# One encoder layer on one core: matmul operands moved to multiples of 256 bytes, sums of weights and ready blocks issued at other places

## The chip, the cores and the metric

One Trainium2 chip, of which the kernel uses one core. The metric is the device time of one execution in microseconds (us). TensorE (PE), VectorE (DVE), ScalarE (ACT), GpSimd (POOL) and SyncE (SP, here a DMA queue) run their own instruction streams.

## The reference

One layer of an encoder with 512 tokens of 2048 channels, in fp32:

```python
h = rms_norm(x, pre_mix)
z = h @ w_in                              # q | k | v | u, 1024 columns each
a = chunked_attention(q, k, v, rel_bias)  # 8 heads of 128, chunks of 64, own chunk and 8 before
p = pooled(u) - u, a linear map per group, a scale per channel   # trailing means over 2, 4, 8, 16
x = x + rms_norm(concat(a, p) @ w_o, post_mix)
h = rms_norm(x, pre_ffn)
up = dwconv3(h @ w_up)                    # 2 x 5632 columns
x = x + rms_norm((gelu(up[:, :5632]) * up[:, 5632:]) @ w_down, post_ffn)
```

## The kernel before

Every fp32 matrix product is made of matmuls in a reduced fp32 format: `split` (L138) writes an operand as a rounded part (ACT, L140, names ending in h) and a rest (DVE, L141, names ending in l). `mm3` (L161) multiplies rounded by rounded, rounded by rest and rest by rounded; `mm2` (L167) does the same with one 512-wide matmul (L170) and one 256-wide matmul (L176) for two halves packed in one operand, all eight wide ones of a product and then all eight narrow ones, or in the other order for products that are "turned".

Large products go by a scheme with seven products of sums of blocks in place of eight. It needs sums of weight blocks and sums of activations. The stages, in time: q and k of the first head, to 31 us; half of v; q and k of heads 1 to 7 by seven products each (class Pairs, L432), to about 205 us, whose activation sums s5, s3, s6 lie in pool `ph`; then attention head by head between the second half of v, u and the pooling, to about 400 us; w_o by seven products (`wo_product`, L848, order 1, 7, 2, 5, 6, 3, 4, each twice for `cc` 0 and 1, in four quarters `q`); three blocks of w_up in the plain way; from about 632 to 1438 us the other 41 blocks of w_up by seven products (class Factors, L1320), whose activation sums h5, h3, h6 (`h` in the profile) lie in a pool named `ps` and whose plain factors `gT` lie in `big`; from 1438 us w_down by seven products in chunks (`multiply`, L1147), whose right factors `bh`, `bl` lie partly in pool `p4`, partly in pool `pr`; and a last block `yl`, from 1827 us.

Pools are laid out by a stack from the left and one from the right of the 128 partitions' memory. `place` (L100) allocates a tile that nothing reads, to shift all that comes behind it in its stack. Where matmul operands lie in the built program, as byte address in the partition modulo 256: `big` (the weights' parts `w4`, the plain factors, the factors of w_o), `p4`, `acc` and `p1`'s attention tiles at 128; `ps`, `pr` and `p1`'s `dh` at 0; `ph` at 224. Of 9564 matmuls, 6158 have both operands at 128, 3070 have the moving one at 0 and the stationary one at 128, 336 have the moving one at 224 and the stationary one at 128. The factors in `ps`, `pr` and `ph` are moving operands.

The order on PE is that of the code. The other engines are ordered by a scheduler, in which program order, buffers and `issue_after` count. `weights` (class Weights, L55) loads blocks through SP (L152) and splits them a few blocks ahead of their use.

The sums of weights for w_o and for the first chunk of w_down are made in DRAM by DMA alone, in `sums_in_dram` (L290): 48 steps, each a copy (L301 on POOL, L304 on SP) or an adding transfer (L308 on POOL) of 1 MB; steps 1 to 32 are for w_o, 33 to 48 for w_down. `more_sums(n)` takes the next n steps where the code calls it. While `more_sums.paced` is set, the copies too go through POOL's queue, and each step is held back by a memset on DVE (L295) and one on POOL (L296), so that it starts at that place in time. Step 6 is taken in the first half of v, 26 by the end of q and k, 28, 30 and 32 by the ends of heads 0, 1 and 2, 43 by the end of u, 46 in w_o and 48 in w_up.

Six blocks of w_down's first chunk are split ahead of time, in w_o (`ready_block`, L837): load a block `rw` through SP (L840), split it (`rwh`, L843) and store both parts in DRAM (L846). Each of the products 5, 6 and 3 of w_o starts one at its first quarter, both for `cc` 0 and 1, loads it behind quarter 0, splits it behind quarter 2 and stores it behind quarter 3.

Of the kernel before, what the change touches and what calls it, by code (L numbers as in the profile page):

```python
# [9 lines left out]
F32 = mybir.dt.float32  # L10
F32R = mybir.dt.float32r
# [4 lines left out]
P = 128  # L16
# [18 lines left out]
PAD = 16  # L35
# [10 lines left out]
def f32(ap):  # L46
    return ap.bitcast(F32)
# [34 lines left out]
def encoder_layer(ctx: ExitStack, tc: tile.TileContext, x, xT, vecs, rel, post_mix, post_ffn,  # L82
# [7 lines left out]
    nc = tc.nc  # L90
    ctx.enter_context(tc.manual_schedule(engines={mybir.EngineType.PE}))

    const = ctx.enter_context(tc.tile_pool(name="const", bufs=1))
# [6 lines left out]
    def place(pool, n):  # L100

        pool.tile([P, n // 4], F32, tag="place", bufs=1, name="place")

    place(const, 224)

    def bank(name):
        return psum.tile([P, 512], F32, tag="ps", name=name)
# [30 lines left out]
    def split(hi, lo, src, scale=None):  # L138
        if scale is None:
            rounded = nc.scalar.activation(hi, src, AF.Copy)  # L140
            rest = nc.vector.tensor_sub(lo, src, f32(hi))  # L141
        else:
            rounded = nc.scalar.activation(hi, src, AF.Copy, scale=scale)
            rest = nc.vector.scalar_tensor_tensor(lo, src, scale, f32(hi), op0=ALU.mult, op1=ALU.subtract)
        split.last, split.rest = rounded.ins, rest.ins
        return rounded.ins
# [109 lines left out]
    def first_block(cc, j, l):  # L256
        cs = slice(l * D // 2 + cc * S, l * D // 2 + (cc + 1) * S)
        return w_down[:2 * P * CU, cs].rearrange("(u j p) n -> p u j n", j=2, p=P)[:, :, j, :]

    READY = (0, 1), (1, 1), (0, 2)  # L260
    ready_w = {at: [dram.tile([P, CU, S], F32, name=f"rw{at[0]}{at[1]}{p}") for p in "hl"] for at in READY}

    ready_parts = [(at, j) for at in READY for j in range(2)]
# [65 lines left out]
    def more_sums(n):  # L329
        for _ in range(n):  # L330
            next(sums_step, None)
# [6 lines left out]
    rt = const.tile([P, NT], F32, name="rt")  # L338
    T = S // 2
    hsum, early_x, mixing_w = (ctx.enter_context(ExitStack()) for _ in range(3))  # L340
    ph = hsum.enter_context(tc.tile_pool(name="ph", bufs=1, side="right", reuse_waits="tile"))
    px = early_x.enter_context(tc.tile_pool(name="px", bufs=1, reuse_waits="tile"))
    ms = {i: ph.tile([P, 8, 2, T], F32R, tag=f"s{i}", name=f"s{i}") for i in (5, 3, 6)}
# [7 lines left out]
    for kb in range(KD):  # L351
        i, o = divmod(kb, 8)
        nc.sync.dma_start(xt[kb // 4][:, kb % 4, :], xT[kb * P:(kb + 1) * P, :])
        for n, what in enumerate("qk"):
            if kb in chunks:
                raw, hi, lo = first[f"{what}0_{i}"]
# [5 lines left out]
        for what in "qk":  # L362
            _, hi, lo = first[f"{what}0_{i}"]
# [132 lines left out]
    pairs = Pairs()  # L496
    psv = [bank(f"v0_{t}") for t in range(NT)]
    sums_of_x = x_sums()
    for n, _ in enumerate(v_steps(0, psv)):
        if n in (3, 5, 7, 9, 11, 13):  # L500
            more_sums(1)
        for _ in range(2):
            next(sums_of_x, None)
        if n == 9:
            for i, v in enumerate(differences):
                split(*(hT[i][:, :, at, :] for at in AT[1]), v)
            early_x.close()
            p0 = mixing_w.enter_context(tc.tile_pool(name="p0", bufs=1, reuse_waits="tile"))
# [75 lines left out]
    for k, i in [at for at in pairs.order if at[0] is not None]:  # L584
        if k == pairs.n - 1 and i in (7, 4):
            if not steps:
                psv = [bank(f"v1_{t}") for t in range(NT)]
                steps = v_steps(1, psv)
            next(steps)
        qk_product(k, i)  # L590
        qk_keep(k, i)
        if (k, i) == pairs.order[2]:
            spread1()
        if (k, i) == (pairs.n - 1, 7):
            restore()
            state["z", 0] = raw4("zq0").rearrange("p (a b) -> p a b", a=2)
            nc.sync.dma_start(state["z", 0], zqk[0])
            state["bias", 0] = raw4("bias0")[:, :S]
            restore.last = nc.sync.dma_start(state["bias", 0], rel[0]).ins
        if i in ((3, 7, 4) if k < pairs.n - 1 else (7, 4)):  # L600
            more_sums(1)

    hsum.close()
# [8 lines left out]
    with tc.tile_pool(name="p1", bufs=2, reuse_waits="tile") as p1:  # L612
# [110 lines left out]
        def pool_keep(g, j, ps):  # L723
            w = WINDOWS[g]
            u = p1.tile([P, WIDE], F32, tag="u", bufs=1, name="u")[:, :PAD + S]
            nc.vector.memset(u[:, :PAD], 0.0)
            nc.vector.tensor_mul(u[:, PAD:], ps, R)
            cur, step = u, 1
            while step < w:
                nxt = p1.tile([P, WIDE], F32, tag="us", bufs=2, name="us")[:, :PAD + S]  # L730
                nc.vector.tensor_add(nxt[:, step:], cur[:, step:], cur[:, :PAD + S - step])
                if 2 * step < w:
                    nc.vector.memset(nxt[:, :step], 0.0)
                cur, step = nxt, 2 * step
            edge = p1.tile([P, PAD], F32, tag="uf", bufs=2, name="uf")
            nc.vector.tensor_mul(edge, cur[:, PAD:2 * PAD], recip[:, g, :])
            d = t512("tmp", bufs=1)
            nc.vector.tensor_sub(d[:, :PAD], edge, u[:, PAD:2 * PAD])
            nc.vector.scalar_tensor_tensor(d[:, PAD:], cur[:, 2 * PAD:], 1.0 / w, u[:, 2 * PAD:],
                                           op0=ALU.mult, op1=ALU.subtract)  # L740
            hi, lo = t512(f"dh{j}", F32R, 1), t512(f"dl{j}", F32R, 1)
            split(hi, lo, d)
            state["pool", g, j] = hi, lo
# [25 lines left out]
        for h in range(3):  # L769
            if not h:  # L770
                run(2)
                ready_head(0)
            run(1)
            scores(h)
            more_sums(1)
            run(1)
            if h:
                values(h - 1)
            more_sums(1)
            run(1)  # L780
            ready_head(h + 1)
            run(1)
            turn(h)
            if not h:
                v_ready()
# [3 lines left out]
        def mid(h):  # L789
            def step():  # L790
                values(h)
                more_sums(1)
                if h == 2:
                    scores(3)
                elif h + 2 < HEADS:
                    ready_head(h + 2)
                if h == 3:
                    v_load(1)
            return step

        for j in range(8):
            ps = project(f"u{j}", mid(2 if j == 0 else j + 1) if j not in (1, 7) else None)
            if j == 0:
                ready_head(4)
            if j == 2:
                v_ready()
            if 1 <= j <= 5:
                turn(j + 2)
                if j < 5:
                    scores(j + 3)  # L810
            if j in (2, 4, 6):
                pool_mix(j // 2 - 1, spill_mix)
            if j < 7:
                pool_keep(j // 2, j % 2, ps)
                more_sums(1 if j in (0, 1, 3, 5, 6) else 0)
        u7 = ps
        more_sums.paced = False
        weights.ahead = 4
# [15 lines left out]
                split(*(w[:, 4 * i:4 * i + 4, :] for w in parts), v)  # L834
            return parts

        def ready_block(at, j):  # L837
            v, hi = (p2.tile([P, 1024], dt, tag=tag, name=tag) for tag, dt in (("rw", F32), ("rwh", F32R)))
            lo = v.bitcast(F32R)
            nc.sync.dma_start(v.rearrange("p (a b) -> p a b", a=2), first_block(at[0], at[1] - 1, 0)[:, 2 * j:2 * j + 2, :])  # L840
            yield
            yield
            split(hi, lo, v)  # L843
            yield
            for dest, part_ in zip(ready_w[at], (hi, lo)):
                nc.sync.dma_start(dest[:, 2 * j:2 * j + 2, :], f32(part_).rearrange("p (a b) -> p a b", a=2))  # L846

        def wo_product(i, cc, left, between=None):  # L848
            ps = [bank(f"m{i}{cc}{t}") for t in range(2)]
            if cc and i in (1, 5, 6):  # L850
                more_sums(1)
            ready = ready_block(*ready_parts.pop(0)) if i in (5, 6, 3) else iter(())
            for q in range(4):
                w = weights.get(f"wo{i}_{cc}_{q}")
                for j in range(2):
                    kb = 2 * q + j
                    for t in range(2):
                        mm3(ps[t], tuple(v[:, kb, t * P:(t + 1) * P] for v in left), part(w, j), kb == 0, kb == 7)
                next(ready, None)
                if between:  # L860
                    between(q)
            return ps
# [12 lines left out]
    with tc.tile_pool(name="p2", bufs=1, reuse_waits="tile") as p2:  # L875
# [164 lines left out]
                gate_part(q - 1, 2)  # L1040
                weights.prefetch(q)
        keep_x(2, turn_back.last)
        more_sums.paced = True
        for q in range(4):
            w = weights.get(f"w10_{q}")
            if q in (0, 2):
                more_sums(1)
            for kb in range(4 * q, 4 * q + 4):
                for j in range(2):
                    mm3(ups[1][j], part(w, j, slice(kb % 4 * P, (kb % 4 + 1) * P)), g_both(hT, kb),  # L1050
                        kb == 0, kb == KD - 1)
# [443 lines left out]
    with tc.tile_pool(name="p4", bufs=2, reuse_waits="tile") as p4:  # L1495
# [68 lines left out]
        ready = []  # L1564
# [111 lines left out]
        for n in ("11", "12", "21", "22"):  # L1676
            for t in range(2):
                at = y[t + 2 * int(n[0]) - 2]
# [64 lines left out]
```

## Time and profile before

| | us |
|---|---|
| median of 3 runs | 1878.97 |
| lowest and highest | 1877.44, 1880.14 |
| the profiled execution | 1881.62 |
| its span, first to last instruction | 1879.9 |

The mean granted clock of TensorE is 0.998 of full. In the timeline, a row has the start, the duration, the engine, the line, the operation, out<-in, sizes and count; in brackets the engine's idle time ahead and what ended it. The start-to-start distance of two PE rows, divided by the matmuls between them, is the rate of PE; the duration of one is longer than that, since matmuls overlap. A row of the chain has a start, a duration and the work. Groups of a tile have the lowest, median and highest duration in ns, and the first and last start.

### The profile page before, as it was taken

The numbers are of one execution on the slowest core, as the hardware profiler recorded it, in microseconds if no ns is written. First come the engines' busy times: TensorE is split into PE (matmuls) and PEld (weight loads), VectorE is DVE, ScalarE is ACT, GpSimd is POOL, SyncE is SP. The second block draws the span as 40 slices with busy tenths as digits, with TensorE's granted clock in tenths as the row PEclk, the third lists the DMA queues.
The fourth block names the chain that finished last, engine by engine and source line by source line (L and its number), as shares of the span: only waits on it lengthen the run. The fifth ranks groups of instructions, "written<-read, shape, count | busy, mean of one in ns | idle before, by whom it ended". The sixth has DMA issues, their size and how long they took to land.

```text
span 1879.9 us, 25452 instructions
## 1 busy us (share of the span) xinstructions
PE 1860.0 (99%) x9598; PEld 1584.6 (84%) x9598; DVE 1539.7 (82%) x1805; ACT 1082.1 (58%) x1376; POOL 303.3 (16%) x403
## 2 busy tenths in 40 slices
PE   9999999999999999999999999999999999999998
PEld 7888878887888888888888888888888888888886
DVE  6987767887698988888888888888888899898876
ACT  8655454556565656666566665656655655555453
POOL 3311110000000121212212122121121011111101
PEclk9999999999999999999999999999999999999999
DMA  7699997798985888888888988898888967777785
GB/s 284 193 319 305 311 267 213 225 251 300 347 297 183 213 197 199 206 207 200 196 197 206 208 196 197 202 207 207 195 177 297 360 215 160 192 212 170 171 238 143
DMA packets 139338, 426.01 MB, mean 227 GB/s; under 512 B 11920, under 2 KB 15376, under 8 KB 133520
## 3 DMA queue, kind: packets, MB, share of 16 engines
q0 software_dynamic: 54864, 173.56, 46.1%
q1 hardware_dynamic: 84352, 250.84, 38.1%
q8 instruction: 75, 1.23, 0.3%
q14 instruction: 47, 0.39, 0.1%
HBM read 370.35 MB, written 104.33 MB: 253 GB/s over the span
## 4 chain that ended last, share of the span: by engine, by line
PE 88%; DMA 4%; DVE 4%; ACT 2%; issue 1%; SPq 0%; POOL 0%; DVEq 0%; POOLq 0%; ACTq 0%
PE qa L170 18%; PE qa L176 9%; PE qg L170 9%; PE qg L176 5%; PE qd L170 4%; PE pa L162 4%; PE pa L164 4%; PE pa L165 4%; PE qd L176 2%; PE pg L162 2%; PE pg L164 2%; PE pg L165 2%; PE m L164 2%; PE m L165 2%; PE m L162 2%; PE u L162 1%
## 5 line engine op out<-in xcount | busy, mean ns | idle before, releaser
L140 ACT ACTIVATE wfh<-wx 128x1024 fp32r<-128x1024 f32 x192 | 203.6, 1060 | 151.7 <-PE qg L170 57.6
L170 PE MATMUL qa<-gT,wfh 128*128 128x512 f32 x1152 | 289.1, 393 | 0.0
L141 DVE TENSOR_TENSOR wfl<-wx,wfh 128x1024 fp32r<-128x1024 f32 x192 | 234.7, 1223 | 64.0 <-ACT wfh L140 46.7
L170 PEld LDWEIGHTS qa<-gT,wfh 128*128 128x128 f32 x1152 | 207.0, 188 | 37.5
L1360 POOL DMA_DIRECT2D wx<-in_w_up x122 | 104.6, 857 | 498.6 <-DVE wfl L141 468.3
L140 ACT ACTIVATE wfh<-wy 128x1024 fp32r<-128x1024 f32 x96 | 101.9, 1061 | 120.1 <-PE qg L170 62.4
L170 PE MATMUL qg<-h,wfh 128*128 128x512 f32 x656 | 165.7, 394 | 0.0
L176 PE MATMUL qa<-gT,wfl 128*128 128x256 f32 x1152 | 160.8, 282 | 1.7 <-ACT zm L1420 1.7
L176 PEld LDWEIGHTS qa<-gT,wfl 128*128 128x128 f32 x1152 | 151.0, 190 | 6.5 <-ACT zm L1420 2.1
L170 PEld LDWEIGHTS qg<-h,wfh 128*128 128x128 f32 x656 | 122.9, 188 | 28.0
L141 DVE TENSOR_TENSOR bl<-b,bh 128x2048 fp32r<-128x2048 f32 x56 | 127.3, 2287 | 22.5 <-ACT bh L140 11.7
L140 ACT ACTIVATE bh<-b 128x2048 fp32r<-128x2048 f32 x56 | 105.8, 1912 | 49.2 <-DVE b L1118 20.5
L141 DVE TENSOR_TENSOR wfl<-wy,wfh 128x1024 fp32r<-128x1024 f32 x96 | 117.2, 1221 | 13.3 <-ACT wfh L140 6.5
L162 PE MATMUL pa<-bh,ah 128*128 128x512 f32 x320 | 126.1, 394 | 0.0
L164 PE MATMUL pa<-bl,ah 128*128 128x512 f32 x320 | 125.8, 393 | 0.0
L165 PE MATMUL pa<-bh,al 128*128 128x512 f32 x320 | 125.5, 392 | 0.0
L141 DVE TENSOR_TENSOR wfl<-wz,wfh 128x1024 fp32r<-128x1024 f32 x48 | 58.7, 1224 | 53.7 <-PE qa L170 52.5
L176 PEld LDWEIGHTS qg<-h,wfl 128*128 128x128 f32 x656 | 89.4, 188 | 7.5
L170 PE MATMUL qd<-gT,wfh 128*128 128x512 f32 x384 | 95.7, 391 | 0.0
L176 PE MATMUL qg<-h,wfl 128*128 128x256 f32 x656 | 91.6, 282 | 0.0
L170 PEld LDWEIGHTS qd<-gT,wfh 128*128 128x128 f32 x384 | 72.0, 188 | 16.2
L170 PE MATMUL qa<-h,wfh 128*128 128x512 f32 x328 | 83.2, 395 | 0.0
(550 smaller groups left out, 4364.5 us busy)
## 6 DMA issues: line engine op xcount, KB each, us to landing
wx<-in_w_up POOLq DMA_DIRECT2D x122, 512.0 KB, 6.4
b<-in_w_down SPq DMA_DIRECT2D x32, 1024.0 KB, 6.9
wt<-in_w_o POOLq DMA_DIRECT2D x24, 1024.0 KB, 17.2
wx<-in_w_up SPq DMA_DIRECT2D x43, 512.0 KB, 5.5
wz<-in_w_up SPq DMA_DIRECT2D x41, 512.0 KB, 5.6
wy<-in_w_up SPq DMA_DIRECT2D x41, 512.0 KB, 4.4
wy<-in_w_up POOLq DMA_DIRECT2D x41, 512.0 KB, 6.7
sum<-part POOLq DMA_DIRECT2D x38, 512.0 KB, 6.1
```

The lines of the kernel that those rows point to most:

```text
L140: rounded = nc.scalar.activation(hi, src, AF.Copy)
L141: rest = nc.vector.tensor_sub(lo, src, f32(hi))
L162: nc.tensor.matmul(ps, l[0], r[0], start=first, stop=False, skip_group_check=onto)
L164: nc.tensor.matmul(low, l[0], r[1], start=False, stop=False, skip_group_check=onto)
L165: nc.tensor.matmul(ps, l[1], r[0], start=False, stop=last, skip_group_check=onto)
L170: nc.tensor.matmul(ps, w[0][:, kb], pairs[kb][0], start=fresh and not kb, stop=last, skip_group_check=not fresh)
L176: nc.tensor.matmul(ps[:, sl], w[1][:, kb], pair[:, sl], start=False, stop=last, skip_group_check=not fresh)
L1360: nc.gpsimd.dma_start(self.raw[k, what], self.block(k, m, kh), accum_op=ALU.add)
```

## The change

Three parts. **Placement:** the tile that shifts the left stack is 96 bytes in place of 224, a new one of 224 bytes stands ahead of `ph` on the right, and the pooling's `edge` tile has four buffers of 64 bytes in place of two. In the built program, all 9564 matmuls then have both operands at 0 mod 256: `big`, `p4` and `acc` move down by 128 bytes, `ph` from 180192 to 179968; `ps` and `pr` stay at 179968, which is 256 mod 512, while `big` and `p4` are at 0 mod 512.

**Sums:** calls of `more_sums` move. Step 7 is taken in the first half of v; no step is taken in the last product of q and k nor in head 0; two are taken in the attention of heads 3 and 4, and one behind each of the seven u blocks; the two paced steps in w_up are gone. 25 steps are taken by the end of q and k, 25, 27 and 29 by the ends of heads 0, 1 and 2, 44 by the end of u, and the last four (two copies through SP, two adding transfers through POOL) in w_o, one each in products 2, 5, 6 and 3.

**Ready blocks:** one generator goes through the six blocks over all products of w_o but the first: load, split four quarters later, store one quarter later, next block two quarters later.

```diff
-    place(const, 224)
+    place(const, 96)
...
+    place(hsum.enter_context(tc.tile_pool(name="place_ph", bufs=1, side="right")), 224)
     ph = hsum.enter_context(tc.tile_pool(name="ph", bufs=1, side="right", reuse_waits="tile"))
...
     for n, _ in enumerate(v_steps(0, psv)):
-        if n in (3, 5, 7, 9, 11, 13):
+        if n in (1, 3, 5, 7, 9, 11, 13):
             more_sums(1)
...
-        if i in ((3, 7, 4) if k < pairs.n - 1 else (7, 4)):
+        if i in (3, 7, 4) and k < pairs.n - 1:
             more_sums(1)
...
-            edge = p1.tile([P, PAD], F32, tag="uf", bufs=2, name="uf")
+            edge = p1.tile([P, PAD], F32, tag="uf", bufs=4, name="uf")
...
             scores(h)
-            more_sums(1)
+            if h:
+                more_sums(1)
             run(1)
             if h:
                 values(h - 1)
-            more_sums(1)
+                more_sums(1)
...
                 values(h)
-                more_sums(1)
+                more_sums(2 if h in (3, 4) else 1)
...
-                more_sums(1 if j in (0, 1, 3, 5, 6) else 0)
+                more_sums(1)
...
-        def ready_block(at, j):
-            v, hi = (p2.tile([P, 1024], dt, tag=tag, name=tag) for tag, dt in (("rw", F32), ("rwh", F32R)))
-            lo = v.bitcast(F32R)
-            nc.sync.dma_start(v.rearrange("p (a b) -> p a b", a=2), first_block(at[0], at[1] - 1, 0)[:, 2 * j:2 * j + 2, :])
-            yield
-            yield
-            split(hi, lo, v)
-            yield
-            for dest, part_ in zip(ready_w[at], (hi, lo)):
-                nc.sync.dma_start(dest[:, 2 * j:2 * j + 2, :], f32(part_).rearrange("p (a b) -> p a b", a=2))
+        def ready_blocks():
+            for at, j in ready_parts:
+                v, hi = (p2.tile([P, 1024], dt, tag=tag, name=tag) for tag, dt in (("rw", F32), ("rwh", F32R)))
+                lo = v.bitcast(F32R)
+                nc.sync.dma_start(v.rearrange("p (a b) -> p a b", a=2),
+                                  first_block(at[0], at[1] - 1, 0)[:, 2 * j:2 * j + 2, :])
+                for _ in range(4):
+                    yield
+                split(hi, lo, v)
+                yield
+                for dest, part_ in zip(ready_w[at], (hi, lo)):
+                    nc.sync.dma_start(dest[:, 2 * j:2 * j + 2, :], f32(part_).rearrange("p (a b) -> p a b", a=2))
+                for _ in range(2):
+                    yield
+
+        ready_steps = ready_blocks()
...
-            if cc and i in (1, 5, 6):
+            if cc and i in (2, 5, 6, 3):
                 more_sums(1)
-            ready = ready_block(*ready_parts.pop(0)) if i in (5, 6, 3) else iter(())
...
-                next(ready, None)
+                if i != 1:
+                    next(ready_steps, None)
...
-        more_sums.paced = True
         for q in range(4):
             w = weights.get(f"w10_{q}")
-            if q in (0, 2):
-                more_sums(1)
```

PE's order is the same in both kernels. On POOL, before, the queue from the last sum of q and k to the start of head 1 reads as follows (`wt` are the sums for w_o in DRAM, `recip` a table of the pooling, which is made between q and k and head 0; the copies `wt40<-wt60` and `wt41<-wt61` are steps 25 to 28):

```order
L308 DMA wt61_99<-in_w_o 128x4x512
L618 MEMSET recip_2091 128x16 x4
L620 MEMSET recip_2091 128x1 x26
L296 MEMSET pace_2033 128x1
L301 DMA wt40_100<-wt60_98 128x2048
L296 MEMSET pace_2077 128x1
L301 DMA wt40_100<-wt60_98 128x2048
L296 MEMSET pace_2240 128x1
L301 DMA wt41_101<-wt61_99 128x2048
L296 MEMSET pace_2256 128x1
L301 DMA wt41_101<-wt61_99 128x2048
```

After, at the same place in the program:

```order
L308 DMA wt61_99<-in_w_o 128x4x512
L296 MEMSET pace_1922 128x1
L301 DMA wt40_100<-wt60_98 128x2048
L619 MEMSET recip_2092 128x16 x4
L621 MEMSET recip_2092 128x1 x26
L296 MEMSET pace_2391 128x1
L301 DMA wt40_100<-wt60_98 128x2048
L296 MEMSET pace_2421 128x1
L301 DMA wt41_101<-wt61_99 128x2048
L296 MEMSET pace_2555 128x1
L301 DMA wt41_101<-wt61_99 128x2048
```

The first of the four copies stands ahead of the table now; the other three are held back to heads 1 and 2. On ACT, before, where product 5 of w_o follows product 2 (`wo5_0_0h` is the first block of product 5, `rwh` a ready block):

```order
L140 ACTIVATE wo2_1_2h_4322<-wo2_1_2r_4284 128x1024
L140 ACTIVATE wo2_1_3h_4340<-wo2_1_3r_4302 128x1024
L140 ACTIVATE rwh_4642<-rw_4641 128x1024
L140 ACTIVATE wo5_0_0h_4362<-wo5_0_0r_4320 128x1024
L140 ACTIVATE wo5_0_1h_4380<-wo5_0_1r_4338 128x1024
L140 ACTIVATE wo5_0_2h_4398<-wo5_0_2r_4360 128x1024
L140 ACTIVATE wo5_0_3h_4416<-wo5_0_3r_4378 128x1024
```

After:

```order
L140 ACTIVATE wo2_1_2h_4340<-wo2_1_2r_4302 128x1024
L140 ACTIVATE wo2_1_3h_4358<-wo2_1_3r_4320 128x1024
L140 ACTIVATE wo5_0_0h_4383<-wo5_0_0r_4338 128x1024
L140 ACTIVATE wo5_0_1h_4403<-wo5_0_1r_4356 128x1024
L140 ACTIVATE wo5_0_2h_4421<-wo5_0_2r_4381 128x1024
L140 ACTIVATE rwh_4438<-rw_4437 128x1024
L140 ACTIVATE wo5_0_3h_4442<-wo5_0_3r_4401 128x1024
```

The ready block's rounding has moved from ahead of `wo5_0_0h` to behind `wo5_0_2h`.

## The prediction

> **What bounds the kernel now.** The page comes first: the busy line, then the shares of the chain of work that ended last.
>
> ```profile
> span 1879.9 us, 25452 instructions
> PE 1860.0 (99%) x9598; PEld 1584.6 (84%) x9598; DVE 1539.7 (82%) x1805; ACT 1082.1 (58%) x1376; POOL 303.3 (16%) x403
> PE 88%; DMA 4%; DVE 4%; ACT 2%; issue 1%; SPq 0%; POOL 0%; DVEq 0%; POOLq 0%; ACTq 0%
> ```
>
> TensorE is busy for 99% of the span, and the kernel's PE order is the same before and after, row by row. So time can come from two places only: the few gaps in PE's row, and the time from one matmul's start to the next. The instruction's own duration (0.39 us) says nothing of the second, since matmuls overlap; I subtract starts in the PE timeline. First in w_o, then twice in w_down:
>
> ```profile
> 487.70 0.39 PE L162 MATMUL m<-wo_3h,n 128*128 128x512 f32 x1
> 490.42 0.39 PE L162 MATMUL m<-wo_0h,s 128*128 128x512 f32 x1
> ```
>
> ```profile
> 1501.22 0.39 PE L162 MATMUL pa<-bh,ah 128*128 128x512 f32 x1
> ...
> 1505.30 0.40 PE L162 MATMUL pa<-bh,ah 128*128 128x512 f32 x1
> ...
> 1511.60 0.39 PE L162 MATMUL pa<-bh,ah 128*128 128x512 f32 x1
> ```
>
> Between the w_o rows lie 12 matmuls: 2.72 / 12 = 226.7 ns each. From 1501.22 to 1505.30 there are 18, again 226.7 ns. From 1505.30 to 1511.60 there are 27, of the same shape, tile names and line, at 233.3 ns. What differs is the buffer that the moving operand (`bh`, `bl`) lies in: in the first product it is in pool p4, which starts 128 bytes past a multiple of 256 like the stationary operand; from 1505.30 on it is in pool `pr` on the right side, at a multiple of 256. The same pairing (moving at 0, stationary at 128 mod 256) occurs in a pool of the left side, p1's `dh`, which the pooling map multiplies:
>
> ```profile
> 420.44 0.40 PE L162 MATMUL pm<-dh,pm3h 128*128 128x512 f32 x1
> ...
> 423.24 0.39 PE L162 MATMUL m<-wo_0h,s 128*128 128x512 f32 x1
> ```
>
> Twelve matmuls in 2.80 us, 233.3 ns. So it isn't the side of the memory: where the two operands stand unlike mod 256, a 512-wide matmul costs about 6 ns more; where alike, it settles at 226.7. The rows cannot tell "unlike" from a period of 512, since all alike pairs of this kernel are also alike mod 512.
>
> **Part 1, placement.** It puts all operands at a multiple of 256: the stationary ones and big, p4, acc move down by 128, `ph` by 224, while `ps` and `pr` stay. *w_down and the last block* run from the first to the last of these rows:
>
> ```profile
> L162 PE MATMUL pa<-bh,ah x320: 389/393/404, 1438.7 to 1826.4; 128*128 128x512 f32 x160
> ...
> L162 PE MATMUL yl<-wb,gh x68: 277/392/404, 1827.1 to 1871.0; 128*128 128x512 f32 x60, 128*128 128x256 f32 x8
> ```
>
> ```profile
> 1440.00:1800.00 360.00, 360.00 (x1559) 292.38 (x1558) 315.04 (x203) 210.52 (x199) 40.07 (x37) 1.00 0.78 215
> ```
>
> The window row (us, PE busy and count, then PEld, DVE, ACT, POOL, clock, DMA share, GB/s) has 1559 matmuls less one or two that began before it: 360 / 1557.5 = 231.1 ns on average, a mixture of 226.7 and 233.3. At 226.8 for all, 432.5 us x 4.3 / 231.1 = **-8.0**. The DMA share there is 0.78 and PE never stops, so the loads have the room.
>
> *Factors* (41 periods of seven products, from about 632 to 1438 us), one period by the chain and by its sets of eight:
>
> ```profile
> 1000.92 1.89 PE qa L176 x16
> 1020.53 1.89 PE qa L176 x16
> ```
>
> ```profile
> 1002.65 2.03 PE L170 MATMUL qa<-h,wfh 128*128 128x512 f32 x8
> 1004.51 1.99 PE L170 MATMUL qd<-gT,wfh 128*128 128x512 f32 x8
> 1006.34 1.11 PE L176 MATMUL qd<-gT,wfl 128*128 128x256 f32 x8
> ...
> 1008.26 2.00 PE L170 MATMUL qa<-gT,wfh 128*128 128x512 f32 x8
> 1010.10 2.02 PE L170 MATMUL qg<-h,wfh 128*128 128x512 f32 x8
> 1011.96 1.12 PE L176 MATMUL qg<-h,wfl 128*128 128x256 f32 x8
> ```
>
> The period is 19.61. Sets with `h` (pool `ps`, unlike) take 1.86 (1002.65 to 1004.51; 1010.10 to 1011.96), `gT` (alike) 1.84 behind a narrow set and 1.83 behind an `h` set, against 8 x 0.2267 = 1.813. The switch from 256 to 512 wide itself costs alike pairs 1.84 - 1.813 = 0.03, and that stays: four sets of seven follow a narrow one. After: 4 x 1.84 + 3 x 1.813 = 12.80 in place of 12.94 (1.86 three times, 1.84 twice, 1.85, 1.83); the narrow sets, 6.67 us, gain about 0.02 back. 19.49 instead of 19.61: 41 x -0.12 = **-4.9**. The same products in *q and k of heads 1 to 7* (moving operands in `ph`, at 224 mod 256):
>
> ```profile
> 107.84 1.91 PE qa L176 x16
> 127.53 1.91 PE qa L176 x16
> ```
>
> 19.69, and 19.49 after by the same sets: 7 x -0.20 = **-1.4**. Part 1 in all is -14.3; its bounds are nothing and -20, if the switches' 0.03 went too (48 periods x 4 sets x 0.03 = 5.8).
>
> A rule of the Trainium skill speaks against this part. Its page "SBUF — State Buffer", section "Operand start alignment", asks only that an operand start at a multiple of its element size and calls that a matter of legality, not speed; under "SBUF: two separate sides" TensorE has ports of its own that never wait. [...]
>
> **Part 2, copies away from the first head.** The one long gap of PE:
>
> ```profile
> 240.90 0.28 PE L165 MATMUL s<-qkh,qkl 128*128 128x256 f32 x1
> 244.99 0.53 PE L162 MATMUL s<-qkh 128*128 128x384 f32 x1 [3.82 <-DVE ptl L141]
> ...
> 248.51 0.45 PE L162 MATMUL v<-v_0h,gT 128*128 128x512 f32 x1
> ```
>
> ```profile
> 245.00:250.00 5.00, 5.00 (x16) 4.04 (x17) 4.55 (x14) 2.84 (x5) 2.73 (x4) 0.66 0.92 267
> ```
>
> ```profile
> 242.02 1.06 ACT L140 ACTIVATE v_3h<-v_3r 128x1024 fp32r<-128x1024 f32 x1 [5.39 <-DMA v_3r<-in_w_v]
> ```
>
> ```profile
> 221.18 20.77 DMA v_3r<-in_w_v
> ```
>
> PE waits for DVE's `ptl`, which waits behind ACT, which waited 5.39 us for the load of `v_3r`, 20.77 us on its way. The gap is 244.99 - 240.90 - 0.12 = 3.97. Behind it the clock is halved (0.66 over the window): nine matmuls take 3.52 instead of 3 x 0.174 + 6 x 0.2267 = 1.88, 1.64 more. Together 5.6. The load's company on the queues:
>
> ```profile
> 218.98 0.57 POOL L301 DMA_DIRECT2D wt<-wt  x1
> ...
> 226.89 0.52 POOL L301 DMA_DIRECT2D wt<-wt  x1
> ```
>
> ```profile
> DMA to landing us min/median/max: 6.9/13.8/20.8
> ```
>
> These are the first and the last of four, at 218.98, 221.06, 226.35 and 226.89, each a copy of 1 MB in DRAM. The change moves one ahead (beside QK) and the rest behind this head. The other load of `v_3r` took 6.9 us. ACT comes free 242.02 - 5.39 = 236.6, so anything under 15.4 us closes the gap. Between 6.9 and 20.8 I take the unloaded end, since all four copies go: **-5.6**, bounds 0 and -5.6. The copies then fall beside heads 1 and 2, which had two each before and have two each now.
>
> **Part 3, blocks spread over w_o.** PE's next largest gap is where product 5 begins:
>
> ```profile
> 458.27 1.10 SPq L840 DMA_DIRECT2D rw<-in_w_down  x1
> ```
>
> ```profile
> 465.20 1.06 ACT L140 ACTIVATE rwh<-rw 128x1024 fp32r<-128x1024 f32 x1 [7.43 <-issue]
> 466.16 1.04 ACT L140 ACTIVATE wo_0h<-wo_0r 128x1024 fp32r<-128x1024 f32 x1
> ```
>
> ```profile
> 466.54 0.39 PE L165 MATMUL m<-wo_3h,a 128*128 128x512 f32 x1
> 467.26 0.50 PE L162 MATMUL m<-wo_0h,n 128*128 128x512 f32 x1 [0.33 <-ACT wo_0h L140]
> 468.71 0.50 PE L164 MATMUL m<-wo_0l,n 128*128 128x512 f32 x1 [0.95 <-DVE wo_0l L141]
> ```
>
> The block's rounding is queued ahead of `wo_0h` and ACT sits 7.43 us until the load, issued at 458.27, has landed. PE loses 467.26 - 466.54 - 0.227 = 0.49 and 468.71 - 467.26 - 0.227 = 1.22. In the new order `rwh` stands three roundings later, and there are four quarters (4 x 2.72 = 10.9 us) between load and rounding instead of two; loads of these blocks took 6.9 and 8.82 us:
>
> ```profile
> 426.24 8.82 DMA rw<-in_w_down
> ```
>
> So **-1.7**, bounds 0 and -1.7. Queued behind a late block are ACT's next `wo` rounding, its DVE rest and PE; the roundings are made three ahead, which is the cover.
>
> **What is added.** Steps 47 and 48, 1 MB sums that stood in w_up, now run in w_o, where the queues are full:
>
> ```profile
> 480.00:520.00 40.00, 40.00 (x178) 33.14 (x177) 27.47 (x24) 20.13 (x22) 0.00 (x0) 1.00 0.93 349
> ```
>
> They lengthen the loads beside them. The trace has no such pair in w_o; the nearest row is the 1.7 us stall for one late load, so bounds 0 and two of those, 3.4 (with a late copy beside the u blocks, 4). PE is at 40.00 of 40.00 there at a share of 0.93 already, so I take **+1.0**. The doubled `edge` tile costs 128 bytes and no instruction.
>
> Sum: -14.3 - 5.6 - 1.7 + 1.0 = -20.6. The profiled execution, 1881.62, becomes 1861.0; it lay 2.65 above the median of the runs, so the median goes from 1878.97 to 1858.4.
>
> **Rivals.**
> (a) *The offset is worth nothing*, since the period is 512 and `ps`, `pr` stay at 256 mod 512 against stationary operands at 0, or since it is something else of these pools. For: no row separates 256 from 512. Against: `dh` on the left side. Then -5.6 - 1.7 + 1.0 = -6.3: 1872.7. [...]
> (b) *Slower: it is the odd 128 under both operands that lets them settle*, and at 0 all take the unlike pace. Its place is every wide matmul that now stands at 226.7: about 400 us in q, v, u, w_o and w_up x 6 / 227 = 10.6; a third of w_down (the mean 231.1 between 226.7 and 233.3), 144 us x 6 / 227 = 3.8; four `gT` sets of some 0.025 in 48 periods, 4.8. That is +19.2, with the -6.3 of the other parts +12.9: 1891.9. It decides if the w_o rows after stand above 231 ns; from 2 ns per such matmul (6.3 / 19.2 x 6) it outweighs the other parts. For: no pair of this kernel is alike at 0. Against: a bare start address would have to matter more than the pair's relation, and `ps`, `pr` at 0 already have the slow pace only beside operands at 128.
> (c) *Alignment works, the gaps only move* (the copies meet another load, the added sums stall w_o as much): -14.3 + 1 = 1865.7.
>
> **How the numbers follow.** Forecast 0.61, (a) 0.22, (c) 0.07, (b) 0.10. The likeliest alone lies between 1855 and 1866. To hold 8 in 10 the range takes in (c) and (a) with its added waits: 1852 to 1875; outside are (b), some of (a) with its gaps kept, and a little below. A measurement of this kernel tells about 0.2%, 3.8 us, from no change. Faster by more: the forecast, (c) and most of (a), 0.85; within: the rest of (a), 0.05; slower: (b), 0.10.
>
> **What would show it.** Right: 226.7 ns in w_down with `pr`, a Factors period of 19.49, no gap at the first head with `v_3r` landing within 15 us, no idle ACT ahead of `wo_0h` of product 5. Wrong: 233 ns still in w_down but 226.7 in w_o (a); over 231 in w_o (b); new gaps of 1 us or more at heads 1 and 2 or in w_o (c).

## The result and the profile after

| | median us | lowest to highest | runs |
|---|---|---|---|
| before | 1878.23 | 1877.44 to 1880.14 | 4 |
| after | 1858.47 | 1857.2 to 1859.2 | 4 |

Before has a fourth run here, so its median is not the 1878.97 of the prediction. The ratio is 0.9893, with a 95% interval of 0.9875 to 0.9910. The profiled execution of after took 1859.2 us. Its page:

```profile
span 1857.4 us, 25457 instructions
PE 1843.6 (99%) x9598; PEld 1584.8 (85%) x9598; DVE 1540.8 (83%) x1804; ACT 1082.3 (58%) x1376; POOL 303.2 (16%) x402
PE 93%; DMA 3%; DVE 2%; ACT 1%; issue 1%; SPq 0%; DVEq 0%; POOL 0%; POOLq 0%; ACTq 0%
```

The span is 22.5 us shorter, and PE is busy for 16.4 us less with the same 9598 matmuls: they follow each other faster. The other 6.1 us are time in which PE was not busy; its share of the chain rises from 88 to 93%.

The pace, in the PE timeline of after, for the two products of w_down shown of before (the first with its right factor in `p4`, the second, from 1489.82 on, in `pr`):

```profile
1484.38 0.39 PE L162 MATMUL pa<-bh,ah 128*128 128x512 f32 x1
...
1489.82 0.39 PE L162 MATMUL pa<-bh,ah 128*128 128x512 f32 x1
...
1495.94 0.39 PE L162 MATMUL pa<-bh,ah 128*128 128x512 f32 x1
```

24 matmuls in 5.44 us and 27 in 6.12: 226.7 ns in both, where the second had 233.3. The same window of w_down as before:

```profile
1440.00:1800.00 360.00, 360.00 (x1590) 298.20 (x1589) 320.57 (x205) 213.07 (x203) 40.37 (x37) 1.00 0.79 217
```

1590 matmuls in place of 1559, at the same DMA share (0.79 and 0.78). One period of Factors, by the chain, and its sets of eight:

```profile
988.06 1.91 PE qa L176 x16
1007.55 1.91 PE qa L176 x16
```

```profile
989.81 2.00 PE L170 MATMUL qa<-h,wfh 128*128 128x512 f32 x8
991.65 1.98 PE L170 MATMUL qd<-gT,wfh 128*128 128x512 f32 x8
993.47 1.11 PE L176 MATMUL qd<-gT,wfl 128*128 128x256 f32 x8
```

19.49 in place of 19.61; the set behind a narrow one takes 1.84, the one behind a wide set 1.82. At the first head, PE, ACT and the tile's loads:

```profile
239.08 0.28 PE L165 MATMUL s<-qkh,qkl 128*128 128x256 f32 x1
239.20 0.34 PE L162 MATMUL s<-qkh 128*128 128x384 f32 x1
```

```profile
234.72 1.04 ACT L140 ACTIVATE v_3h<-v_3r 128x1024 fp32r<-128x1024 f32 x1
```

```profile
DMA to landing us min/median/max: 7.2/8.2/9.2
```

PE goes on after 0.12 us; no load of `v_3r` takes over 9.2 us, and ACT does not wait for it. At product 5 of w_o:

```profile
457.61 0.39 PE L165 MATMUL m<-wo_3h,a 128*128 128x512 f32 x1
457.83 0.39 PE L162 MATMUL m<-wo_0h,n 128*128 128x512 f32 x1
458.06 0.39 PE L164 MATMUL m<-wo_0l,n 128*128 128x512 f32 x1
```

No gap. The program on PE is the same row by row, so the start of the same matmul in two traces divides the whole difference by stages. The table has the forecast's term and the measured differences from before, in us; the two columns to the right belong to the first two experiments below.

| from one start to another | forecast | after | placement alone | the rest alone |
|---|---|---|---|---|
| up to the first product of q and k of heads 1 to 7 | 0 | -0.04 | +0.05 | +0.21 |
| q and k of heads 1 to 7 (133.21 before) | -1.4 | -1.74 | -1.26 | -0.51 |
| from there to the gap of the first head | 0 | -0.04 | -0.05 | 0.00 |
| the gap and nine matmuls behind it (7.90) | -5.6 | -5.64 | -0.01 | -5.64 |
| from there to the end of u (149.89) | 0 | -1.40 | +0.21 | +0.30 |
| w_o to the end of product 2 (67.85) | 0 | -0.07 | +0.01 | -0.08 |
| start of product 5 (2.51) | -1.7 | -1.83 | -1.01 | -1.83 |
| rest of w_o (78.49) | +1.0 | +1.64 | -0.03 | -0.06 |
| to the end of the plain blocks of w_up (84.94) | 0 | +0.37 | -0.36 | +0.18 |
| Factors (806.25) | -4.9 | -5.44 | -6.29 | -1.88 |
| w_down and the last block (432.56) | -8.0 | -8.21 | -8.21 | 0.00 |
| sum | -20.6 | -22.40 | -16.95 | -9.31 |

### The profile page after: what moved, and what is told of

The parts are those of the page before. It is cut to its first block, busy times and chain, and to the rows that moved or that the text cites. A ratio compares the mean times of both kernels' runs of the same rounds, so it can differ in the third digit from the quotient of the medians.

```text
span 1857.4 us, 25457 instructions
## 1 busy us (share of the span) xinstructions
PE 1843.6 (99%) x9598; PEld 1584.8 (85%) x9598; DVE 1540.8 (83%) x1804; ACT 1082.3 (58%) x1376; POOL 303.2 (16%) x402
## 4 chain that ended last, share of the span: by engine, by line
PE 93%; DMA 3%; DVE 2%; ACT 1%; issue 1%; SPq 0%; DVEq 0%; POOL 0%; POOLq 0%; ACTq 0%
PE qa L170 18%; PE qa L176 10%; PE qg L170 9%; PE qg L176 5%; PE qd L170 4%; PE pa L164 4%; PE pa L165 4%; PE pa L162 4%; PE qd L176 2%; PE pg L164 2%; PE pg L165 2%; PE pg L162 2%; PE m L164 2%; PE m L165 2%; PE m L162 2%; PE v L164 2%
```

## The experiments

Each was run beside the kernel before on the same chip; a ratio is that of the kernel to before, with its 95% interval.

### Placement alone, and the rest alone

The first is the kernel before with

```diff
-    place(const, 224)
+    place(const, 96)
+    place(hsum.enter_context(tc.tile_pool(name="place_ph", bufs=1, side="right")), 224)
```

and the second is the kernel after with these lines undone. The pooling's `edge` tile is in neither: in the built programs the 48 matmuls of `dh` stay unlike in the first and are alike in the second, about 0.3 us at 6 ns each.

> The kernel before with the placement alone (left tile 96 bytes, 224 bytes ahead of ph). Theory (the pace of a wide matmul hangs on whether its two operands start alike modulo 256): -14.5 us, as the trace after divides it: q and k of heads 1 to 7 -1.7, Factors about -4.6, w_down and the last block -8.2; the gap of 4 us at the first head and the 1.7 us at product 5 of w_o stay. Rival (the pace follows from the lighter DMA load of the other two parts, not from the addresses): within 2 us of before, w_down still with 233 ns per matmul on the right factors.

> The changed kernel without its placement (sums and ready blocks as after, addresses of big, p4, acc and ph as before). Theory: -7.5 us: first head -5.6, product 5 -1.7, the gap at the u blocks (322 us) -1.1, new gaps in w_o +1.2, two waits on zm in Factors -2, one new one +1; w_down still at 231 ns on average. Rival: the two halves are not additive, since the gaps of Factors move with the pace of PE: -4 to -5 us here.

Placement alone: 1864.64 against 1876.59 us, ratio 0.9932 (0.9920 to 0.9945), about -12.8 us. The rest alone: 1872.36, ratio 0.9975 (0.9966 to 0.9984), -4.7 us. 0.9932 x 0.9975 is 0.9907, inside the interval of the whole. The window of w_down, of placement alone and of the rest alone:

```profile
1440.00:1800.00 360.00, 360.00 (x1590) 298.20 (x1589) 319.97 (x202) 214.03 (x203) 40.75 (x37) 1.00 0.78 217
```

```profile
1440.00:1800.00 360.00, 360.00 (x1560) 292.44 (x1559) 312.77 (x197) 209.63 (x198) 39.18 (x36) 1.00 0.77 211
```

1590 as after, 1560 as before: w_down's gain is the placement's, whole, and the rest gives none of it. The load of `v_3r` with placement alone, in the chain of waits:

```profile
219.91 20.45 DMA v_3r<-in_w_v
```

It is as late as before, and the gap costs the same 7.89 us in all. So by time the two halves are additive, and the theory on the pace holds. Both gains are smaller than expected, though: -12.8 where -14.5 was expected, and -4.7 where -7.5 was. The -4.7 is the number that the rival gave, although its reason, halves that are not additive, is not what the ratios show.

The stage differences are larger than the times: -16.95 and -9.31, together -26.3 where after has -22.4. All of them are taken from one execution of before, which at 1881.62 us lay 5.0 above the median of before beside these two kernels. Some of that stands in waits which other executions lack: the two on `zm` (1.07 and 0.95) and about 1.0 of the 1.83 at product 5 are gone with placement alone too, which touches no transfer there, so they weren't the moved sums' doing. The other 2 us are not placed.

### Sums alone, and blocks alone

The kernel before with the moved calls of `more_sums` and nothing else, and with `ready_blocks` and nothing else (both as in the diff of the change).

> The kernel before with the moved sums alone. Theory: v_3r lands in time, the 4 us gap and the half clock at the first head go: -5.6 us, and the two waits on zm early in Factors go with the two sums that leave w_up (-2 us); w_o gets two sums more beside the bunched ready blocks, up to +2. About -6 us. Rival: the load of v_3r is late for its own queue's sake and lands after 240 us here too: within 1 us of before.

> The kernel before with the spread ready blocks alone. Theory: the 1.7 us at the start of product 5 go, and some 1.2 us come back between 515 and 535 us, where ACT still waits for a block and five roundings come at once: -0.5 us, not to be told from 0 by the time, only by the trace. Rival (the new gaps of w_o after come from the two added sums, not from the blocks): -1.7 us and no gap over 0.3 us in w_o.

Sums alone: 1873.68, ratio 0.9987 (0.9978 to 0.9996); blocks alone: 1874.07, ratio 0.9990 (0.9982 to 0.9999). Together 0.9977, as the rest alone. `v_3r`'s loads with the sums alone, and the late one with the blocks alone:

```profile
DMA to landing us min/median/max: 6.8/7.4/8.0
```

```profile
220.33 19.76 DMA v_3r<-in_w_v
```

The sums alone close the gap, and its stretch of PE goes from 7.90 to 2.26 us, as after. That is -5.6, but the time is only 2.4 us shorter. PE waits anew in w_o, whose part behind product 5's start takes 81.60 us in place of 78.49:

```profile
PE m L164 <- DVE wo_3l L141: 2.5, 2, 1.5
```

These 3.1 us do not explain all of it: the two traces still differ by 8.2 us, of which 5.0 is again that the profiled execution of before lay above its median.

With the blocks alone that part takes 78.43 and has no gap, nor has product 5's start. So the added sums load w_o, and the spread blocks take that away, all of it in the rest alone (78.43) and about half in after (80.13): of the first pair of theories, the return of a gap with the blocks alone did not come, and the rival (the new gaps come from the added sums) holds.

The gap at the start of product 5 goes with either half (2.51 to 0.68 us), in two ways. ACT at product 5's blocks, first with the sums alone, then with the blocks alone:

```profile
457.42 1.06 ACT L140 ACTIVATE wo_2h<-wo_2r 128x1024 fp32r<-128x1024 f32 x1 [2.54 <-DMA wo_2r<-wt]
464.87 1.06 ACT L140 ACTIVATE rwh<-rw 128x1024 fp32r<-128x1024 f32 x1 [6.39 <-DMA rw<-in_w_down]
```

```profile
460.74 1.06 ACT L140 ACTIVATE rwh<-rw 128x1024 fp32r<-128x1024 f32 x1 [5.45 <-DMA rw<-in_w_down]
461.71 1.04 ACT L140 ACTIVATE wo_0h<-wo_0r 128x1024 fp32r<-128x1024 f32 x1
```

The sums alone already put the rounding behind product 5's first three blocks, the order that the kernel after has. The blocks alone leave it ahead of them, as before, but issue its load earlier: at 453.90, 11.0 us ahead of the last matmul before product 5 (464.91), where before had 8.3 (458.27 and 466.54).

### Where the common start may lie

All operands at 128 and at 64 mod 256, and `ps` and `pr` moved away from the rest, all from the kernel after:

```diff
# all at 128
-    place(const, 96)
+    place(const, 224)
-    place(hsum.enter_context(tc.tile_pool(name="place_ph", bufs=1, side="right")), 224)
+    place(hsum.enter_context(tc.tile_pool(name="place_ph", bufs=1, side="right")), 96)
-    place(ctx.enter_context(tc.tile_pool(name="place", bufs=1, side="right")), 224)
+    place(ctx.enter_context(tc.tile_pool(name="place", bufs=1, side="right")), 96)
# all at 64: 160 in the three places
# unlike: left as after, 208 ahead of ph (0 mod 256 in the built program, as after),
# 160 ahead of ps (64 mod 256), 32 more ahead of pr (32 mod 256)
```

> The changed kernel with every operand 128 bytes off: left tile 224, right tile ahead of ph and ahead of ps 96 each, so that all 9564 matmuls have both operands at 128 mod 256. Theory (only the relation of the two operands counts): as after, 226.7 ns in w_down on all right factors, within 3 us of after (-18 to -21 us from before). Rival (an operand must start at a multiple of 256): at least the 10 us that w_down and Factors gained come back.

> The changed kernel with every operand at 64 mod 256 (left tile 160, right tiles 160). Theory: as after again, 226.7 ns and -18 to -21 us from before. Rival (the common start must be a multiple of 128, as in every fast pair so far): all wide matmuls at 229 to 235 ns, 15 us or more slower than after.

> The changed kernel with the right pools moved apart: ps at 64 and pr at 32 mod 256, the left operands at 0 and ph nearly as after. Theory (any unlike start costs, whatever its size, since 128 and 96 cost 6 and 7 to 8 ns): w_down on pr and Factors on ps fall back to the pace of before, 8 and 4 us, so about 12 us slower than after. Rival 1 (the cost grows with the distance between the starts): a half or less of that. Rival 2 (only a distance of about half the period hurts): as after.

All at 128: 1858.37, ratio 0.9905 (0.9890 to 0.9920). All at 64: 1859.16, 0.9909 (0.9894 to 0.9924). Unlike: 1870.10, 0.9962 (0.9948 to 0.9976). The window of w_down, for all at 64 and for unlike:

```profile
1440.00:1800.00 360.00, 360.00 (x1590) 298.20 (x1589) 322.57 (x207) 213.85 (x203) 41.57 (x38) 1.00 0.78 219
```

```profile
1440.00:1800.00 360.00, 360.00 (x1556) 291.66 (x1555) 312.14 (x198) 208.93 (x197) 39.18 (x36) 1.00 0.77 210
```

1590 for any common start, 1556 where `pr` stands 32 bytes off. No multiple of 256 is needed, only that both operands start alike modulo 256; since `ps` and `pr` lie 256 off the rest modulo 512 after, the period is not 512. From the start of w_down to the last matmul, the unlike kernel takes 433.72 us against 424.35 after: 9.4 for 32 bytes, more than the 8.2 that 128 bytes cost. Factors, with `ps` 64 bytes off, takes 802.90 against 800.81, or 800.41 in the second execution below: 2 to 2.5 for 64, where before had some 4 to 5 for 128. So the cost doesn't grow with the distance, which ends rival 1; but 64 is cheaper than 32 and 128, against the theory's "whatever its size".

### The kernel after once more

> The changed kernel itself, once more, for what differs between two executions. Theory: the pace of the matmuls repeats to within 0.1 us per stage (Factors and w_down between gaps), while the gaps of PE in w_o (1.2 us), at 1374 us (1.1 us) and on zm come and go by up to 1 to 2 us. Rival: the gaps of w_o stand in the same rows with the same lengths, so they belong to the change.

1857.36, ratio 0.9904 (0.9887 to 0.9921). w_down and the last block take 424.35 us again, to the hundredth. Factors takes 800.41 in place of 800.81, the rest of w_o 79.28 in place of 80.13. The gap of 1.08 us at 1374 us is 0.61. The pace repeats, the gaps come and go. Those of w_o are fewer here but not gone, so neither theory holds as it was put: their place belongs to the change, their length doesn't.

### What is left in w_o

In the trace after, ACT, DVE and PE in product 6:

```profile
500.77 1.06 ACT L140 ACTIVATE rwh<-rw 128x1024 fp32r<-128x1024 f32 x1 [5.22 <-DMA rw<-in_w_down]
501.73 1.05 ACT L140 ACTIVATE wo_1h<-wo_1r 128x1024 fp32r<-128x1024 f32 x1
```

```profile
508.80 1.22 DVE L141 TENSOR_TENSOR wo_3l<-wo_3r,wo_3h 128x1024 fp32r<-128x1024 f32 x1
509.93 2.28 DVE L948 TENSOR_TENSOR y<-y,y 128x2048 f32<-128x2048 f32 x1
512.14 1.22 DVE L141 TENSOR_TENSOR wo_0l<-wo_0r,wo_0h 128x1024 fp32r<-128x1024 f32 x1
```

```profile
512.74 0.39 PE L162 MATMUL m<-wo_0h,s 128*128 128x512 f32 x1
513.41 0.50 PE L164 MATMUL m<-wo_0l,s 128*128 128x512 f32 x1 [0.28 <-DVE wo_0l L141]
```

ACT stands 5.22 us before a late ready block, the `wo` blocks reach DVE late and together, between the sums of `y` of 2.28 us each, and PE starts 0.67 - 0.23 = 0.44 late. Two ways out were tried: a fifth quarter between load and rounding, and the last two sums back in w_up.

```diff
# five quarters
-                for _ in range(4):
+                for _ in range(5):
# late sums
-            if cc and i in (2, 5, 6, 3):
+            if cc and i in (2, 5):
+        more_sums.paced = True
         for q in range(4):
             w = weights.get(f"w10_{q}")
+            if q in (0, 2):
+                more_sums(1)
```

> The changed kernel with five quarters of a w_o product between the load of a ready block and its rounding in place of four (eight steps a block, 48 for six). Theory (what is left of PE's gaps in w_o comes from ACT standing 4 to 5 us before a late block, and five roundings then reach DVE together): no idle time of ACT over 2 us ahead of a block, no gap of PE in w_o, 0 to 1.2 us less than after, which the time can hardly tell. Rival (ACT waits there for the weight blocks wo of its own look-ahead, whatever the ready block does): the same idle times and gaps.

> The changed kernel with its last two sums (steps 47 and 48) back in w_up, held back by memsets as before. Theory (these two adding transfers cost w_o up to 1 us, as forecast): loads of w_o land sooner from 452 us on, ACT waits less ahead of the ready blocks of products 5 and 6; in exchange the waits on zm near 672 and 693 us may come back: -1 to +2 us, near 0. Rival (they are covered everywhere, the prefetch of w_o has room): the same waits of ACT in w_o within 1 us and no difference in time.

Five quarters: 1858.49, ratio 0.9909 (0.9895 to 0.9924), and the theory falls. ACT waits longer (7.05 and 7.64 us where after has 4.10 and 5.22), and the rest of w_o takes 80.97 us, no less than after's 80.13. The chain of waits there shows why:

```profile
484.37 8.03 DMA rw11l<-rw
492.41 0.02 issue
492.42 0.02 SPq L843
492.44 0.03 issue
492.47 4.33 DMA rw<-in_w_down
```

The load of the next block is issued 0.07 us after the last store of the block before has landed: `rw` has one buffer. The distance in quarters is between places in the code; the load itself starts when the stores give the buffer back, and a later rounding makes the stores, and so the next load, later too. After is the same: the store issued at 483.14 lands at 493.14, the load goes at 493.20.

Late sums: 1855.99, ratio 0.9884 (0.9870 to 0.9898). The window from 455 to 525 us, of after and of late sums:

```profile
455.00:525.00 70.00, 69.32 (x303) 56.27 (x302) 48.30 (x41) 36.86 (x46) 1.15 (x1) 1.00 0.99 340
```

```profile
455.00:525.00 70.00, 70.00 (x310) 57.99 (x309) 51.65 (x43) 38.27 (x46) 0.00 (x0) 1.00 0.93 324
```

Without the two sums the DMA share falls from 0.99 to 0.93, ACT waits 0.80 us instead of 5.22 for the fifth block, PE has no gap, and the rest of w_o takes 78.43 us, where five runs with these sums and the spread blocks (after, its repeat, all at 128, all at 64, unlike) take 79.10 to 80.61. So the sums cost w_o 0.7 to 2.2 us there, and the rival falls. The rest alone, with the same sums and blocks, took 78.43 too. Its matmuls run no slower in w_o than those of after (67.8 us to the end of product 2 in both), so their pace is not the reason; why its one profiled execution has no gap is open. The median of late sums is the lowest of all, but its interval and that of after overlap, so it isn't shown to be the faster kernel.

### Half blocks with two buffers

Twelve blocks of half the size; two `rw` of half the size, which take the memory of one; `rwh` halved and single. Once with the sums as after, once with late sums.

```diff
+                loaded[n] = p2.tile([P, 512], F32, tag="rw", name="rw", bufs=2)
+                nc.sync.dma_start(loaded[n], first_block(cc, j - 1, 0)[:, k, :])
...
+            for n in range(len(halves) + 1):
+                if n < len(halves):
+                    load(n)
+                if n:
+                    v = loaded.pop(n - 1)
+                    made = p2.tile([P, 512], F32R, tag="rwh", name="rwh"), v.bitcast(F32R)
+                    split(*made, v)
+                if 0 < n < len(halves):
+                    yield
+                if n:
+                    store(n - 1, made)
+                for _ in range(3):
+                    yield
```

> The changed kernel with twelve half blocks in place of six ready blocks, and two buffers of half the size for the load (the same memory): load of half n four quarters ahead of its rounding, the stores one quarter behind the rounding, the next load three quarters behind the stores. Theory (a block's load is late because its only buffer is given back by the stores of the block before, 0.02 to 0.06 us ahead of the load's issue in the trace after and in the run with five quarters): loads are issued before the last stores land, ACT waits under 2 us ahead of any rwh, no gap of PE in w_o; 0 to 1.5 us less than after. Rival (the transfers of w_o are simply slow at a DMA share of 0.99, whatever the buffer): ACT still waits 3 to 7 us ahead of some rwh.

> The same with steps 47 and 48 of the sums back in w_up, held back by memsets. Theory: w_o without idle time of PE, as in the run with late sums and whole blocks, so the halves add nothing there: 0 to 2 us less than after. Rival (shorter rows and twice as many transfers cost more than they spare): slower than with late sums alone by 1 us or more, with gaps in w_o.

With the sums as after: 1869.18, ratio 0.9958 (0.9944 to 0.9971), 11 us slower than after. ACT now waits for the other buffer, which the stores give back:

```profile
497.59 0.63 ACT L140 ACTIVATE rwh<-rw 128x512 fp32r<-128x512 f32 x1 [9.24 <-DMA rw11h<-rwh]
```

```profile
499.22 0.79 PE L162 MATMUL m<-wo_1h,s 128*128 128x512 f32 x1 [4.69 <-ACT wo_1h L140]
```

PE stands 4.69 us, and its next matmuls come 0.43 us apart (the granted clock is 0.50 from 499 to 503 us). With late sums, the same code takes 1858.92 (0.9911, 0.9898 to 0.9925), and the rest of w_o 78.46 us with no gap. Theory and rival of the first both meet only a part: the single `rwh` took the place of the single `rw`, and at the higher load the stores come too late for it. Of the second, w_o runs without a gap as expected, and the halves add nothing there. But the kernel is slower than late sums with whole blocks, 0.9911 against 0.9884 or about 5 us, each beside before on a chip of its own: the rival's time is met, not its gaps in w_o. Of that, 2.9 us lie in the stretch from the end of w_o to Factors, which takes 86.37 us in the profile, in place of 83.45.

## Why the prediction was right

The forecast was 1858.4 for the median; 1858.47 was measured. By its own steps:

- **Unlike operands cost about 6 ns a matmul.** Shown. Undone, the pace is back (1560 matmuls in the window); done alone, it is whole (1590). w_down gave 8.2 against 8.0. Factors has 19.49 a period as forecast; by gap-free stretches it gave 4 to 5 (with placement alone 6.29, of which 2.0 are the two gaps on `zm`) against 4.9. q and k of heads 1 to 7 gave 1.3 with placement alone against 1.4; the other 0.5 of the 1.74 came with the rest alone too. Rival (b) is out: at 0 the pace is that of 128. The period of 512, on which rival (a) could rest, is excluded by `pr` at 256 mod 512 after. The Trainium skill's "Operand start alignment" ("SBUF — State Buffer"), which the prediction set against this part, says itself that it is about legality, not speed; so 1590 against 1556 in the window does not contradict it. What in the chip makes the pace depend on both starts was not tried.
- **The copies made `v_3r` late.** Shown for the moved sums: 20.8, 20.4 and 19.8 us in the three kernels with the old calls, 9.2 at most where they moved, and the stretch of PE 5.64 shorter every time. The same calls move the adding transfer ahead of the copies as well (203.84 before, 198.48 after), so what the four copies do by themselves was not measured. They cost nothing that shows beside heads 1 and 2.
- **The block ahead of product 5.** The gap went, 1.8 against 1.7, but the mechanism was only half right. Four quarters between load and rounding are not had, since the load waits for its buffer (451.20 issued, 458.60 rounded). What helped in after is that the rounding stands behind product 5's first blocks, and that order comes with the moved sums, not with the spread blocks, to which the prediction gave the whole term. Some 1.0 of the 1.8 was missing with placement alone too, so the size belongs in part to the one execution of before.
- **Two sums more in w_o.** +1.0 was forecast for the rest of w_o, +1.64 measured in the profile of after and +0.8 in its repeat. With late sums it is nothing, so the mechanism is as put, and the bounds of 0 to 4 held.
- **Not in the sum:** the gap of 1.0 us at 322 us, which went wherever the sums were moved; one of 0.5 to 1.6 us near 346, in five of the eleven runs with moved sums and in none of the three without; the waits on `zm`; a gap at 1374 us.

The gaps come and go by 1 to 2 us between executions of one kernel, and the terms were read from an execution of before that lay above its median. By time, placement gave 12.8 against the forecast's 14.3, and the rest 4.7 against 6.3; the repeat of the whole on another chip gave 0.9904, about 18.0 us against 20.6. That the median was met to a tenth is luck by 2 to 3 us.

Rival (a) put the kernel without the placement's gain at 1872.7, and the rest alone took 1872.36. That closeness is chance: before took 1876.59 beside it and not 1878.97, so the rest is worth 4.7 and not 6.3.

## What to carry to other kernels

When PE never waits, subtract the starts of its matmuls: a group of the same shape that is 3% slower than another points to where its operands lie, and two `place` tiles were worth more here than all moved transfers. Before a load is put further ahead in the code, look at what issues it: where the row ahead of it is the landing of the last store from its only buffer, more distance in the code makes it later. A transfer taken out of one full stage loads the next: at a DMA share of 0.99, two sums of 1 MB cost w_o 0.7 to 2.2 us, and in the plain part of w_up nothing that the time shows.

## What the runs showed of the hardware

In this kernel a 512-wide matmul settles at 226.7 ns when its moving and its stationary operand start alike modulo 256 bytes, at 0, 64 or 128 (1590 matmuls in the window of w_down each time). It does not at distances of 32, 64, 96 (`ph` before) and 128 bytes, and the cost is uneven: w_down lost 9.4 us at 32 and 8.2 at 128, Factors 2 to 2.5 at 64 and 4 to 5 at 128, q and k 1.3 at 96. Distances under 32 bytes were not tried. Rows with alike operands settle a few matmuls after a change from 256 to 512 columns (a set of eight takes 1.84 us behind a narrow set, 1.82 behind a wide one, where eight at 226.7 ns are 1.81).
